# First layer's squares as TensorE products, and its first norm and layer 0 in one written plan

## The chip, the cores and the metric

The kernel runs on one core of a Trainium2 chip. The time is device microseconds of one execution of the whole program; a median of runs is given, and one execution is profiled besides. TensorE is PE in the rows (PEld is its weight load), VectorE is DVE, ScalarE is ACT, GpSimd is POOL; SP issues most of the DMAs. Each engine carries out its own list of instructions in the order in which they stand, and waits for the others by semaphores.

## The reference

Two transformer layers on 512 tokens of width 1024, all in fp32. Cut to what matters for the first layer:

```python
h = rmsnorm(x, attn_norm[layer])                       # x * rsqrt(mean(x*x) + 1e-6) * g
proj = h @ w_in_even[i]
fq, fk, fv, ff, dq, ckv, dkr, iq, ik, iw = jnp.split(proj, split_points, axis=-1)
log_f = jax.nn.log_sigmoid(ff + b_fox_f[i])
fox_out = fox_attention(fq, fk, fv, log_f)             # 8 causal heads with a decay
c_kv = rmsnorm(ckv, g_ckv[i])                          # rank 128
k_rope, iq, ik, dq = rope(...)                         # rotary part
# dsa: per query the 128 keys with the largest index score
score = einsum('bqh,bqhk->bqk', iw, relu(iq . ik)) * idx_scale
_, sel = lax.top_k(score, topk)                        # topk = 128
dsa_out = softmax(q . [c_kv, k_rope] over sel) @ c_kv @ w_uv    # 8 heads
x = x + concatenate([fox_out, dsa_out]) @ w_out_even[i]
x = x + conv_glu_ffn(rmsnorm(x, ffn_norm[layer]), ...)
```

The second layer has 16 heads of block-sparse attention and the same kind of feed-forward part; a norm ends the program.

## The kernel before

The residual stream lies transposed in SBUF: `xT[:, d]` holds features 128d to 128d+127 on the partitions and the 512 tokens along the row, for d from 0 to 7. Every matmul is made of three fp32r products (`mm3`, L171 to L173): a value is kept as a rounded high half (`xh`, `wh_...`) and the rest (`xl`, `wl_...`), and high by high, low by high and high by low are summed in PSUM. A projection such as `mm_fk1` is 8 feature blocks by 3 products, 24 matmuls of 128x512. The gain of the norm is put into `xh` and `xl` by `prep`; the factor 1/rms of a token is multiplied in afterwards, when the result is read out of PSUM (by RB, or by CR and SR, which are the rotary tables times RB). So projections can start before the norm is known, and their three `mm` banks in PSUM come free only after it.

A weight piece (`chunk`, 512 KB) comes by a DMA of SP, its high half is rounded on ACT (L160), and its low half is a subtraction, on DVE in one instruction (L166, 128x1024) or on POOL in four (L164, 128x256 each). Before the change that is one switch, `lo_on_pool`: DVE for the first four pieces, then POOL for all of layer 0's attention.

The first norm goes like this. ACT squares each `xT[:, d]` (L194, L197, L582), POOL and DVE add the eight squares (L198, L584, L585), PE transposes the sum (`st_n`, L204), DVE reduces it and finds the root by a bit trick and three Newton steps (L206 to L213), PE spreads it over the partitions (`bc_n`, L216), and ACT copies it to RB. The norm of ckv (`st_kv`, `bc_kv`) is of the same form.

The head of the program is in code order: `misc` (index keys, index weights, gates), `iq0`, `iq1`, `ckv`. Then the attention of layer 0 follows PLAN0, a string of steps, each of which writes its instructions on every engine: k, q and v are the projections of a head pair (0 to 3 are fox, 4 to 7 dsa), s00 the scores and the softmax of pair 0's first head, m00 its product with the values, i the index scores of a block of 128 queries, x a quarter of the selection for a block, o a part of the output projection. The selection (`select`, L631 and L632) finds the 128 largest scores by 16 rounds of MAX8 and MATCH_REPLACE8 for each of three query blocks, 48 rounds in all, on DVE; the masks `tmask1` to `tmask3` that come out are wanted by the dsa heads (`prt_d`, from s40 on). The score tiles of a head are four (128 to 512 keys), each read by one DVE instruction with its maximum (L360, `mx_f`, `mx_d`), and the PSUM banks for them are two (tag S), so that PE can be two tiles ahead of DVE.

Of the kernel before, what the change touches and what calls it, by code (L numbers as in the profile page):

```python
# [83 lines left out]
def hybrid_kernel(ctx: ExitStack, tc: tile.TileContext, xT_d, pos_d, const_d, vec_d, w_d, out_d, idx):  # L84
# [182 lines left out]
    def stack_k(y, nm, eng=V):  # L267

        out = []
        for n, t in zip("hl", halves(y, nm, eng)):  # L270
            b = big(f"{nm}_b{n}")
            move(b[LO], t[HI])
            move(b[HI], t[HI])
            move(t[HI], t[LO])
            out += [t, b]
        return out[0], out[1], out[2], out[3]
# [6 lines left out]

    def rope_angles():

        def fl(t):
            return t.rearrange("p b f -> p (b f)")

        def ang_tile(nm, k=1):
            return cp.tile([P, k * NB, 8], F32, name=f"ang_{nm}")  # L290
# [20 lines left out]
        n2 = rnd("n2", hi, BIG / TWO_PI)  # L311
        V.tensor_scalar(fl(t), fl(hi), M2[0], None, op0=OP.mult)
# [31 lines left out]
    def soft(nm, e, q, k, bias, decay=None):  # L344
# [4 lines left out]
        for i in range(NB):  # L349
# [50 lines left out]
    def v_group(nm, late=None):  # L400
# [3 lines left out]
        for c in range(2):  # L404
            wh, wl = chunk(f"{nm}{c}")
# [133 lines left out]
    def attention(pairs, plan, pieces):  # L539
# [3 lines left out]
        for step in plan.split():  # L543
            kind, n = step[0], step[1:]
# [19 lines left out]
    acc = sq_acc(0)  # L564
# [21 lines left out]
    w.append(chunk("iq1"))
    V.tensor_copy(selr[0:96, :P], const[0:96, C_SEL:C_SEL + P])
    V.tensor_copy(selr[96:128, :P], const[64:96, C_SEL:C_SEL + P])
    V.tensor_scalar(selr[:, P:], const[:, C_FSEL:C_FSEL + 8], 0.5, None, op0=OP.mult)
    rope_tables(cs)  # L590
    rstd_main(acc, "n0")
    rope_scaled()

    ym = rope(pmisc, "misc")
    ikh, ikl = big("ik_h"), big("ik_l")
    split(ikh[LO], ikl[LO], ym[LO])
    for t in (ikh, ikl):
        move(t[HI], t[LO])
    kr = big("kr")
    G.memset(kr[0:64].bitcast(F32), 0.0)  # L600
    split(kr[64:96], kr[96:128], ym[64:96])
    iwT = cp.tile([P, NB, 4], F32, name="iwT")
    t = ps("T", "iwps")
    for b in range(NB):
        PE.transpose(t[:, b * P:b * P + P], ym[:, b * P:b * P + P], ident)
    A.activation(iwT, t.rearrange("p (b c) -> p b c", b=NB)[:, :, 104:108], AF.Copy, scale=0.0625)
    iq = [stack_q(rope(proj(f"iq{h}", w[h]), f"iq{h}"), f"iq{h}") for h in range(2)]
# [28 lines left out]
    y = scaled(proj("ckv"), "ckv")  # L636
# [280 lines left out]
```

## Time and profile before

| | us |
|---|---|
| median of 3 runs (lowest, highest) | 1246.13 (1246.01, 1248.02) |
| profiled execution | 1245.54 |
| its span | 1243.8 |
| busy PE / DVE / ACT / POOL | 1211.7 / 812.3 / 556.2 / 357.5 |

The span goes from the first to the last instruction of the trace; the profiled execution's own time is 1.7 us longer. At 256 us of the span PE is in the output projection of layer 0's dsa heads; what comes behind is the feed-forward part of layer 0, layer 1 and the last norm. A view by stages (busy time of each engine in a stretch of the span) and the waits tell which engine ends last in a stage; the share of the whole span does not.

### The profile page before, as it was taken

Reading aid. Unit: us, or ns where it says so; the run is one execution under the profiler, and the core shown is the slowest. Engines: PE = TensorE matmul, PEld = TensorE weight load, DVE = VectorE, ACT = ScalarE, POOL = GpSimd, SP = SyncE. Lnnn points to the kernel's source line nnn. Section 1 sums busy time; section 2 is a strip of 40 time slices with the busy share of each in tenths; the row PEclk is TensorE's granted clock in tenths of the full one; section 3 lists DMA queues with packets and bytes.
Section 4 is the critical chain, followed back from the end, with each engine's and each line's share of the span. In section 5 each row is a group of like instructions: output and inputs, shape, how many; then the busy total and the mean of one; then the engine's idle time right before and its main releaser. Section 6 shows DMA issues by size and latency. Waiting matters only on the chain.

```text
span 1243.8 us, 16808 instructions
## 1 busy us (share of the span) xinstructions
PE 1211.7 (97%) x5996; PEld 1012.4 (81%) x5996; DVE 812.3 (65%) x1489; ACT 556.2 (45%) x969; POOL 357.5 (29%) x394
## 2 busy tenths in 40 slices
PE   6899999999999999999999999999999999999997
PEld 4778788888888888888888898888888888888886
DVE  7899987675555445554677787787655445554455
ACT  5574677644333333333434575575433323333234
POOL 3684667442111111111222332422221111111110
PEclk9999999999999999999999999999999999999998
DMA  5343435132332333323337424422232333333321
GB/s 196 103 132 88 126 98 132 56 100 83 107 102 89 98 102 95 92 92 95 106 99 193 124 77 119 120 65 84 85 102 85 102 103 102 101 87 101 102 85 68
DMA packets 57379, 127.24 MB, mean 102 GB/s; under 512 B 7584, under 2 KB 21024, under 8 KB 57296
## 3 DMA queue, kind: packets, MB, share of 16 engines
q1 hardware_dynamic: 56368, 124.81, 34.3%
q10 hardware_dynamic: 864, 1.17, 0.3%
q8 instruction: 47, 0.77, 0.3%
q14 instruction: 36, 0.29, 0.1%
q0 software_dynamic: 64, 0.20, 0.0%
HBM read 104.13 MB, written 2.10 MB: 85 GB/s over the span
## 4 chain that ended last, share of the span: by engine, by line
PE 85%; DVE 8%; issue 4%; ACT 1%; DMA 1%; POOL 0%; POOLq 0%; ACTq 0%; DVEq 0%
PE mm_g L172 6%; PE mm_g L171 6%; PE mm_g L173 6%; PE mm_u L171 6%; PE mm_u L172 6%; PE mm_u L173 6%; PE mm_d L171 6%; PE mm_d L172 6%; PE mm_d L173 6%; PE t_m L384 1%; DVE tmask L632 1%; DVE m L631 1%; PE mm_mk L171 1%; PE mm_mq L173 1%; PE mm_mk L173 1%
## 5 line engine op out<-in xcount | busy, mean ns | idle before, releaser
L446 POOL TENSOR_TENSOR cv<-cv,gs 128x512 f32<-128x512 f32 x44 | 57.2, 1299 | 546.0 <-ACT gs L445 546.0
L171 PE MATMUL mm_d<-a_h,wh_d 128*128 128x512 f32 (+1 forms) x384 | 142.8, 372 | 0.0
L172 PE MATMUL mm_d<-a_l,wh_d 128*128 128x512 f32 (+1 forms) x384 | 142.6, 371 | 0.0
L173 PE MATMUL mm_d<-a_h,wl_d 128*128 128x512 f32 (+1 forms) x384 | 142.6, 371 | 0.0
L515 DVE TENSOR_TENSOR us<-mm_u,cv 128x512 f32<-128x512 f32 x44 | 30.4, 692 | 168.1 <-PE mm_u L173 132.7
L171 PE MATMUL mm_u<-xh,wh_u 128*128 128x512 f32 x352 | 137.3, 390 | 0.0
L172 PE MATMUL mm_g<-xl,wh_g 128*128 128x512 f32 x352 | 137.2, 390 | 0.0
L173 PE MATMUL mm_u<-xh,wl_u 128*128 128x512 f32 x352 | 137.0, 389 | 0.0
L171 PE MATMUL mm_g<-xh,wh_g 128*128 128x512 f32 x352 | 137.0, 389 | 0.0
L173 PE MATMUL mm_g<-xh,wl_g 128*128 128x512 f32 x352 | 137.0, 389 | 0.0
L172 PE MATMUL mm_u<-xl,wh_u 128*128 128x512 f32 x352 | 136.9, 389 | 0.0
L160 ACT CAST wh_g<-raw_g 128x1024 fp32r<-128x1024 f32 x44 | 46.3, 1053 | 143.8 <-PE mm_g L172 141.6
L512 DVE TENSOR_TENSOR gs<-mm_g,RB 128x512 f32<-128x512 f32 x44 | 30.4, 691 | 118.2 <-PE mm_g L173 115.6
L140 ACT CAST wh_d<-raw_d 128x1024 fp32r<-128x1024 f32 x45 | 47.4, 1053 | 124.0 <-PE mm_u L172 103.7
L173 PEld LDWEIGHTS mm_d<-a_h,wl_d 128*128 128x128 f32 x384 | 72.3, 188 | 12.6
L171 PEld LDWEIGHTS mm_d<-a_h,wh_d 128*128 128x128 f32 x384 | 72.3, 188 | 12.5
L172 PEld LDWEIGHTS mm_d<-a_l,wh_d 128*128 128x128 f32 x384 | 72.3, 188 | 12.4
L172 PEld LDWEIGHTS mm_g<-xl,wh_g 128*128 128x128 f32 x352 | 66.1, 188 | 14.2 <-DVE xl L187 0.7
L173 PEld LDWEIGHTS mm_u<-xh,wl_u 128*128 128x128 f32 x352 | 66.1, 188 | 13.8
L171 PEld LDWEIGHTS mm_g<-xh,wh_g 128*128 128x128 f32 x352 | 66.1, 188 | 13.8
L173 PEld LDWEIGHTS mm_g<-xh,wl_g 128*128 128x128 f32 x352 | 66.1, 188 | 13.7
L171 PEld LDWEIGHTS mm_u<-xh,wh_u 128*128 128x128 f32 x352 | 66.1, 188 | 13.6
(778 smaller groups left out, 3059.3 us busy)
## 6 DMA issues: line engine op xcount, KB each, us to landing
raw_g<-in_w SPq DMA_DIRECT2D x44, 512.0 KB, 3.5
raw_u<-in_w SPq DMA_DIRECT2D x44, 512.0 KB, 3.6
raw_d<-in_w SPq DMA_DIRECT2D x41, 256.0 KB, 2.8
raw_d<-in_w SPq DMA_DIRECT2D x29, 192.0 KB, 2.7
raw_d<-in_w SPq DMA_DIRECT2D x34, 128.0 KB, 2.5
raw_oe<-in_w SPq DMA_DIRECT2D x8, 512.0 KB, 4.2
raw_mq<-in_w SPq DMA_DIRECT2D x8, 512.0 KB, 3.7
raw_mk<-in_w SPq DMA_DIRECT2D x8, 512.0 KB, 4.1
```

What stands on the lines that cost most here:

```text
L140: A.copy(dst_h, src)
L160: A.copy(wh, raw)
L171: PE.matmul(out, ah, bh, start=first, stop=False)
L172: PE.matmul(out, ah, bl, start=False, stop=False)
L173: PE.matmul(out, al, bh, start=False, stop=last)
L384: PE.transpose(t[:, n * P:n * P + P], probs[i][:, j * P:j * P + P], ident)
L446: G.tensor_tensor(cv, cv, gs, op=OP.mult)
L512: V.tensor_tensor(gs, og, RB, op=OP.mult)
L515: V.tensor_tensor(us, ou, cv, op=OP.mult)
L631: V.max(m8, sc)
L632: V.match_replace(sc, m8, sc, -3e38)
```

## The change

- **Squares on PE.** For each block of x, four fp32 products (not split) of a 128x128 block of `xT` with itself are summed over the 8 blocks into one PSUM bank (`st_n0`, 32 matmuls, L635 of the new code). The sums of squares of the tokens are on the diagonals; DVE multiplies by the identity and reduces. The squares on ACT and the sums on POOL and DVE are gone. The root is DVE's reciprocal, ACT's Sqrt and one Newton step.
- **ckv's norm.** The four transposes of its squares and the reduction are replaced by four fp32 products with a column of ones.
- **One plan.** The first norm, `misc`, `iq`, `ckv`, the gates and the whole attention of layer 0 are steps of PLAN0. A step has two digits and flags. New letters: p prepares a block, z squares it, a is the rotary tables, b `misc`, t the norm, w an early weight, r splits `misc`, j is `iq`, c `ckv`, f the gates, d the selectors. x is now an eighth of a selection (2 rounds). The projection fk1 stands before iq1 and ckv.
- **Flags.** g puts a weight's low half on POOL, otherwise it is on DVE; l puts the low half of a result (fq, iq, fk, o) on POOL; e builds the two stacked forms of q by half-height casts and subtractions and saves three DMAs (q2 and q5); w moves the other half of k. In layer 0 seven weights' low halves move from POOL to DVE (fv0's two, fq0, dq0 and three pieces of the output projection), and so do two of the four fk and three of the four o_f low halves.
- From the end of the dsa heads' output projection on (the feed-forward part of layer 0 and all behind it), the lists are the same as before.

```diff
 PLAN0 = (
-    "v0 i1 i2 k0 q0 i3 k1 s00 s01 q1 v2 x10 s10 m00 k2 s11 x11 m01 x12 q2 x13 x20 m10 k3 m11 k4 x21 s20 "
...
+    "p00 p01 p02 a00 p03 z00v z01 p04 p05 z02 p06 z03v p07 z04o z05o b00 z06o z07v a10 w00 a20 t00r j00ls "
+    "k10glw j10 r00 c00 v00 f00 i10 q00l i20 k00g d00 s00 i30 x10 x11 x12 q10g s01 s10 x13 s11 x14 v20g "
+    "m00 m01 k20glw m10 q20eg x20 k30g k40g x15 x21 x16 x22 x23 x24 x17 m11 x25 x30 x31 s20 x32 s21 x33 "
+    "q30g x34 m20 s30 s31 m21l x35 q40 k50gw v40 x26 x27 m30 x36 x37 k60w s40 s41 q50egl m31 q60g m40 s50 "
...
-        if lo_on_pool:
+        if pool:
...
+    def root(sums, y, h, n, flags, ms=None):
...
+        V.tensor_scalar(ms, sums, 1.0 / n, EPS, op0=OP.mult, op1=OP.add)
...
+        elif "r" in flags:
+            V.reciprocal(h, ms)
+            A.activation(y, h, AF.Sqrt)
...
+        for _ in range(1 if "p" in flags or "r" in flags else 3):
...
+    def sums_by_ones(st, sq, first, last):
+
+        nb = st.shape[1] // 2
+        for b in range(nb):
+            PE.matmul(st[:, 2 * b:2 * b + 2], sq[:, b * P:b * P + P], ones, start=first and b == 0, stop=last and b == nb - 1)
...
+    def stack_q(y, nm, flags):
+
+
+        if "e" in flags:
+            q = big(f"{nm}_a"), big(f"{nm}_b")
+            for t, r, o in ((q[0], LO, HI), (q[1], HI, LO)):
+                A.copy(t[r], y[r])
+                V.tensor_tensor(t[o], y[r], t[r].bitcast(F32), op=OP.subtract)
+            return q
+        h, l = halves(y, nm, G if "l" in flags else V)
...
-    for d in range(KT):
-        if d < 4:
-            square(d, acc)
...
+    def first_square(n, flags):
+
+
+        if n == 0:
+            x0["st"] = ps("T", "st_n0")
+        for b in range(NB):
+            s = slice(b * P, b * P + P)
+            PE.matmul(x0["st"][:, s], xT[:, n, s], xT[:, n, s], start=n == 0 and b == 0, stop=n == KT - 1 and b == NB - 1)
...
+    def first_scale(n, flags):
+        st = x0["st"]
+        ms, y, h = (col(f"{c}_n0", NB) for c in ("ms", "y", "h"))
+        d = tmp("diag")
+        V.tensor_tensor(d.rearrange("p (b c) -> p b c", b=NB), st.rearrange("p (b c) -> p b c", b=NB),
+                        ident.rearrange("p (b c) -> p b c", b=1).to_broadcast([P, NB, P]), op=OP.mult)
+        V.reduce_sum(ms, d.rearrange("p (b c) -> p b c", b=NB), axis=mybir.AxisListType.X)
+        root(ms, y, h, D, flags)
+        row_scale(y, spread(y, "n0"), "n0")
+        rope_scaled()
...
+    def latent(flags):
+
+        y = scaled(proj("ckv", x0.get("ckv"), "g" in flags, "S" if "s" in flags else "mm"), "ckv")
+        sq = tmp("sqkv")
+        A.activation(sq, y, AF.Square)
+        st = ps("T", "st_kv")[:, :2 * NB]
+        sums_by_ones(st, sq, True, True)
```

TensorE at the start of the program, before, and then after; `mm_misc` is the first projection and `st_n` the new squares:

```order
L171 MATMUL mm_misc<-xh,wh_misc 128x512
L172 MATMUL mm_misc<-xl,wh_misc 128x512
L173 MATMUL mm_misc<-xh,wl_misc 128x512
L171 MATMUL mm_misc<-xh,wh_misc 128x512
L172 MATMUL mm_misc<-xl,wh_misc 128x512
```

```order
L635 MATMUL st_n_146<-xT 128x128 x4
L174 MATMUL mm_misc<-xh,wh_misc 128x512
L635 MATMUL st_n_146<-xT 128x128 x4
L175 MATMUL mm_misc<-xl,wh_misc 128x512
L176 MATMUL mm_misc<-xh,wl_misc 128x512
L174 MATMUL mm_misc<-xh,wh_misc 128x512
L635 MATMUL st_n_146<-xT 128x128 x16
```

The squares, which need nothing but x itself, stand ahead of and between the first products of `misc`; the last eight follow its end.

VectorE where the first dsa head begins (step s40), before and then after; `tmask3_93` is the selection of the last query block, `mx_d00_0` and `prt_d00` the first dsa head's maxima and masked scores:

```order
L141 TENSOR_TENSOR pt_f30_1l_1923<-t_f30_1_1931,pt_f30_1h_1922 128x384
L360 ISA prt_d00_2027,mx_d00_0_2031<-s_d00_0_2028,cmask_83 128x128
L360 ISA mx_d00_0_2031 128x1
L360 ISA prt_d00_2027,mx_d00_1_2037<-s_d00_1_2034,tmask1_91 128x256
L360 ISA mx_d00_1_2037 128x1
L141 TENSOR_TENSOR dk1_l_1961<-mm_dk1_1955,dk1_h_1960 128x512
L141 TENSOR_TENSOR p3_0_1_95<-t_f30_2_1937,p3_0_0_94 128x256
L360 ISA prt_d00_2027,mx_d00_2_2043<-s_d00_2_2040,tmask2_92 128x384
```

```order
L712 MAX m8_3_1965<-tmask3_93 128x8
L452 TENSOR_TENSOR y_f3_1709<-y_f3_1709,o_f30_1920 64x512
L713 MATCH_REPLACE tmask3_93<-m8_3_1965,tmask3_93 128x512
L416 ISA prt_d00_1988,mx_d00_0_1992<-s_d00_0_1989,cmask_83 128x128
L416 ISA mx_d00_0_1992 128x1
L715 TENSOR_SCALAR tmask3_93<-tmask3_93 128x512
L416 ISA prt_d00_1988,mx_d00_1_1998<-s_d00_1_1995,tmask1_91 128x256
L416 ISA mx_d00_1_1998 128x1
L416 ISA prt_d00_1988,mx_d00_2_2004<-s_d00_2_2001,tmask2_92 128x384
```

The last round of the selection, which before stands some 40 instructions earlier, is now directly ahead of the first dsa scores on VectorE.

TensorE at the same step, before and then after; `s_d00_2` is the third score tile of the first dsa head, `mm_dq` a projection of a later pair's queries:

```order
L393 MATMUL o_f30_1919<-p3_0_0_94,fv1__942 128x256
L384 MATMUL t_f31_0_1990<-const_70,prt_f31_1765 128x128
L280 MATMUL s_d00_2_2040<-dk0_h_1505,dq0_a_1843 128x384
L281 MATMUL s_d00_2_2040<-dk0_l_1506,dq0_a_1843 128x384
L280 MATMUL s_d00_3_2046<-dk0_h_1505,dq0_a_1843 128x512
L281 MATMUL s_d00_3_2046<-dk0_l_1506,dq0_a_1843 128x512
```

```order
L440 MATMUL t_f31_1_2107<-const_70,prt_f31_1746 128x128 x3
L174 MATMUL mm_dq2_2144<-xh_74,wh_dq2_2136 128x512
L175 MATMUL mm_dq2_2144<-xl_75,wh_dq2_2136 128x512
L176 MATMUL mm_dq2_2144<-xh_74,wl_dq2_2137 128x512
L174 MATMUL mm_dq2_2144<-xh_74,wh_dq2_2136 128x512
L175 MATMUL mm_dq2_2144<-xl_75,wh_dq2_2136 128x512
L176 MATMUL mm_dq2_2144<-xh_74,wl_dq2_2137 128x512
L174 MATMUL mm_dq2_2144<-xh_74,wh_dq2_2136 128x512
L175 MATMUL mm_dq2_2144<-xl_75,wh_dq2_2136 128x512
L176 MATMUL mm_dq2_2144<-xh_74,wl_dq2_2137 128x512
L174 MATMUL mm_dq2_2144<-xh_74,wh_dq2_2136 128x512
L333 MATMUL s_d00_2_2001<-dk0_h_1427,dq0_a_1867 128x384
```

Ten of the 24 matmuls of `dq2`, which before come later, are now done before that tile.

## Rows read from the trace of the kernel before

**Rows 1.** The page: busy time of the engines, and busy tenths in 40 slices.
```profile
PE 1211.7 (97%) x5996; PEld 1012.4 (81%) x5996; DVE 812.3 (65%) x1489; ACT 556.2 (45%) x969; POOL 357.5 (29%) x394
...
DVE  7899987675555445554677787787655445554455
```
**Rows 2.** Stages: stretch, then busy us (instructions) per engine, granted clock, DMA share, GB/s.
```profile
44.50:75.00 30.50, 26.76 (x167) 23.21 (x166) 26.25 (x62) 20.08 (x34) 19.31 (x22) 1.00 0.39 105
75.00:100.00 25.00, 23.19 (x138) 19.71 (x138) 24.15 (x73) 14.89 (x30) 20.39 (x26) 1.00 0.57 153
100.00:125.00 25.00, 23.52 (x139) 20.04 (x138) 24.18 (x66) 12.76 (x32) 11.18 (x17) 1.00 0.32 87
125.00:157.00 32.00, 30.80 (x164) 25.09 (x163) 31.11 (x78) 18.62 (x41) 21.50 (x31) 1.00 0.49 128
157.00:175.30 18.30, 18.30 (x106) 15.59 (x105) 14.38 (x43) 13.75 (x36) 9.45 (x14) 1.00 0.24 68
175.30:256.00 80.70, 80.10 (x423) 65.30 (x423) 59.12 (x152) 55.67 (x133) 49.86 (x71) 1.00 0.37 96
```
**Rows 3.** Waits of PE, 0 to 256 us: total, times, longest.
```profile
PE mm_misc L172 <- DVE xl L187: 3.2, 2, 2.5
PE ix L280 <- ACT rl L620: 2.6, 2, 2.3
PE bc_n L216 <- DVE y_n L213: 2.2, 1, 2.2
...
PE s_f L356 <- DVE mx_f L360: 1.0, 2, 0.7
```
**Rows 4.** PE in order of time: start, length, instruction, [idle before].
```profile
6.68 0.79 PE L171 MATMUL mm_misc<-xh,wh_misc 128*128 128x512 f32 x1 [6.68 <-ACT wh_misc L140]
...
14.30 0.80 PE L172 MATMUL mm_misc<-xl,wh_misc 128*128 128x512 f32 x1 [2.54 <-DVE xl L187]
...
17.02 0.63 PE L172 MATMUL mm_misc<-xl,wh_misc 128*128 128x512 f32 x1
17.45 0.44 PE L173 MATMUL mm_misc<-xh,wl_misc 128*128 128x512 f32 x1
...
19.58 0.39 PE L173 MATMUL mm_misc<-xh,wl_misc 128*128 128x512 f32 x1
19.81 0.39 PE L171 MATMUL mm_iq<-xh,wh_iq 128*128 128x512 f32 x1
...
25.16 1.03 PE L338 MATMUL tabT<-const,exp_tab 128*128 128x128 f32 x8
```
**Rows 5.** Weight loads of unsplit fp32 products (two records each) at the end.
```profile
1234.66 0.30 PEld L785 LDWEIGHTS st_n<-ones,acc 128*128 128x128 f32 x2
1234.88 0.30 PEld L786 LDWEIGHTS st_n<-ones,sq 128*128 128x128 f32 x2
```
**Rows 6.** DVE in order of time.
```profile
8.06 1.25 DVE L294 TENSOR_SCALAR ang_n<-ang_r 128x32 f32<-128x32 f32 x1
9.23 0.17 DVE L295 TENSOR_SCALAR ang_n<-ang_n 128x32 f32<-128x32 f32 x1
...
27.86 0.17 DVE L207 TENSOR_SCALAR ms_n<-ms_n 128x4 f32<-128x4 f32 x1
28.06 0.17 DVE L208 TENSOR_SCALAR t_n<-ms_n 128x4 int32<-128x4 int32 x1
...
32.17 0.17 DVE L225 COPY rstd_n<-y_n 128x4 f32<-128x4 f32 x1
```
**Rows 7.** DVE where the counted stretch begins and ends.
```profile
43.89 0.68 DVE L240 TENSOR_TENSOR ry_iq<-ry_iq,rs_iq 128x512 f32<-128x512 f32 x1
44.49 0.68 DVE L245 TENSOR_TENSOR sc_ckv<-mm_ckv,RB 128x512 f32<-128x512 f32 x1
...
175.27 0.55 DVE L360 CUSTOM_DVE_ANT_0 prt_d<-s_d,tmask 128x384 f32<-128x384 f32 x1
```
**Rows 8.** DVE by groups, 44.5 to 175.3 us: busy, mean ns, idle before.
```profile
L141 DVE TENSOR_TENSOR fq_l<-sc_fq,fq_h 128x512 fp32r<-128x512 f32 x4 | 4.0, 1006 | 0.0
...
L141 DVE TENSOR_TENSOR dk_l<-mm_dk,dk_h 128x512 fp32r<-128x512 f32 x2 | 1.4, 684 | 0.0
```
**Rows 9.** ACT and a weight's low half on DVE, in order of time.
```profile
4.88 0.72 ACT L186 ACTIVATE xh<-xT,vec 128x512 fp32r<-128x512 f32 x1 [1.73 <-DMA vec<-in_vec]
...
20.85 1.28 ACT L323 ACT_TABLE_LOAD   x1
...
22.65 1.22 DVE L166 TENSOR_TENSOR wl_iq<-raw_iq,wh_iq 128x1024 fp32r<-128x1024 f32 x1
```

More of the change, by code (lines that the diff above doesn't have):

```diff
@@ L265, in stack_q, with stack_k @@
         return a, l
-    def stack_k(y, nm, eng=V):
+    def stack_k(y, nm, flags):
         out = []
-        for n, t in zip("hl", halves(y, nm, eng)):
+        one, two = (LO, HI) if "w" in flags else (HI, LO)
+        for n, t in zip("hl", halves(y, nm, G if "l" in flags else V)):
             b = big(f"{nm}_b{n}")
[L272 to L276, printed above, removed]
+            move(b[LO], t[one])
+            move(b[HI], t[one])
+            move(t[one], t[two])
+            out += [b, t] if "w" in flags else [t, b]
+        return out
     def scores(out, q, k, e, qs, w, first=True):
@@ L354, in soft @@
             if decay is not None:
-                sel, ck = decay
-                PE.matmul(s[:, :wm], sel.to_broadcast([P, P]), ck[:, :wm], start=True, stop=False)
+                PE.matmul(s[:, :wm], decay.to_broadcast([P, P]), misc["ck"][:, :wm], start=True, stop=False)
             scores(s[:, :wm], q, k, e, qs, wm, decay is None)
@@ L420, in v_group, with out_proj @@
         return v
-    def out_proj(nm, o, done=None, part=range(4)):
+    def out_proj(nm, o, done=None, part=range(4), pool=False):
         for dp in part:
-            wh, wl = chunk(f"{nm}{dp}")
+            wh, wl = chunk(f"{nm}{dp}", pool=pool)
             for e in range(2):
@@ L553, in attention @@
                 if e == 1:
-                    c["out"].append(halves(c["y"], f"o_{c['nm']}", c.get("lo", V)))
+                    c["out"].append(halves(c["y"], f"o_{c['nm']}", G if "l" in flags else V))
             else:
-                pieces[kind](int(n))
+                pieces[kind](int(n), flags)
     values = {}
@@ L586, in hybrid_kernel @@
[L586 to L600, printed above, removed]
@@ L601, in hybrid_kernel @@
-    split(kr[64:96], kr[96:128], ym[64:96])
-    iwT = cp.tile([P, NB, 4], F32, name="iwT")
[L603 to L607, printed above, removed]
+    x0 = {"misc": w}
+    def first_square(n, flags):
+        if n == 0:
+            x0["st"] = ps("T", "st_n0")
+        for b in range(NB):
+            s = slice(b * P, b * P + P)
+            PE.matmul(x0["st"][:, s], xT[:, n, s], xT[:, n, s], start=n == 0 and b == 0, stop=n == KT - 1 and b == NB - 1)
@@ new lines, in first_proj, with early_chunk, misc_split @@
+    def first_proj():
+        x0["misc"] = proj("misc", x0["misc"])
+    def early_chunk(n, flags):
+        nm = ("iq0", "iq1", "ckv")[n // 10]
+        x0[nm] = chunk(nm, pool="g" in flags)
+    iwT = cp.tile([P, NB, 4], F32, name="iwT")
+    misc, iq, ckv = {}, [None, None], []
+    def misc_split():
+        ym = misc["y"] = rope(x0["misc"], "misc")
+        ikh, ikl = big("ik_h"), big("ik_l")
+        split(ikh[LO], ikl[LO], ym[LO])
+        for t in (ikh, ikl):
+            move(t[HI], t[LO])
+        misc["ik"] = ikh, ikh, ikl, ikl
+        kr = misc["kr"] = big("kr")
+        G.memset(kr[0:64].bitcast(F32), 0.0)
+        split(kr[64:96], kr[96:128], ym[64:96])
+        t = ps("T", "iwps")
+        for b in range(NB):
+            PE.transpose(t[:, b * P:b * P + P], ym[:, b * P:b * P + P], ident)
+        A.activation(iwT, t.rearrange("p (b c) -> p b c", b=NB)[:, :, 104:108], AF.Copy, scale=0.0625)
@@ L661, in hybrid_kernel @@
-    V.tensor_tensor(ckt[R], lu[R], ck[R].bitcast(F32), op=OP.subtract)
-    for r in (0, 64):
-        A.copy(ck[r:r + 32], lu[R])
-        V.tensor_copy(ck[r + 32:r + 64], ckt[R])
-    lo_on_pool = True
+    def latent(flags):
[4 more added lines that the diff above has]
+        sums_by_ones(st, sq, True, True)
+        _, bc = rstd_by_ones(st, P, "kv", flags)
+        yn = tmp("ckvn")
+        V.scalar_tensor_tensor(yn, y, vec[:, V_GC:V_GC + 1], bc, op0=OP.mult, op1=OP.mult)
+        ckv.extend(halves(yn, "ckv"))
```

200 lines of the change are left out of this document (111 added, 89 removed), and 3 rows, old and new, of the table PLAN0.

## The prediction, made before the run

> **What bounds the kernel now.** I read the page first: PE is busy for 97% of the span, DVE for 65% [rows 1]. That would make every microsecond of PE work added a microsecond lost. But DVE's row of slices says otherwise for the start: slices 3 to 5 are at 9 [rows 1]. So I read the view by stages next [rows 2]. From 75 to 157 us DVE is busy for 24.15 of 25, 24.18 of 25 and 31.11 of 32 us; it has 2.6 us to spare in 82. PE idles 1.8, 1.5 and 1.2 us in the same stages. From 157 on PE is busy without a gap (18.30 of 18.30, then 80.10 of 80.70) and DVE is at 14.38 of 18.30. So three regimes: a head in which PE waits for data and for the norm, a middle in which DVE is full (the selection, the softmax, the low halves) and PE goes at its pace, and from about 157 us PE alone. Everything behind 256 us is the same list before and after, so only this first part counts, and the question is when PE gets to a fixed point of it. I take the third score tile of the first dsa head, read by DVE at 175.27 [rows 7].
>
> The waits of PE in the head are 3.2 us for `xl`, 2.2 us for the norm (`bc_n`), and a start at 6.68 [rows 3, 4]. In the middle they are small ones, for DVE's maxima (1.0) and for ACT (2.6) [rows 3].
>
> **The head.** `misc` takes PE from 6.68 to 19.81 [rows 4]. At the later step of 0.23 us (19.58 to 19.81) its 24 matmuls would take 5.5 us. The rest is waits and a slow clock: up to 17.45 the step is 0.43 us, the lower of the two levels (1.2 GHz), then 0.23 [rows 4]. PE had run without a gap since 14.30, some 3 us, when the clock rose [rows 4].
>
> Added: 32 fp32 products. Nothing of that shape is in the trace. The nearest row is the unsplit fp32 product of the last norm: two records each, 0.22 us from one product to the next (1234.66 to 1234.88), though with two columns only [rows 5]. For 128 columns the tables' transposes give 1.03/8 = 0.13 us a pass [rows 4]. Two passes are 0.22 to 0.26; I take 0.24, 7.7 us in all. At the lower clock it would be twice that. At no cost they can't be, since PE is in order; four passes would be 0.47 each, 15 us.
>
> The Trainium skill ("FP8 and Floating Point Precision", "TensorE Precision Notes") speaks against the change here: "True FP32: 4 passes through PE array". By that the squares would take the 15 us of the upper bound. The trace shows two records per product, so I go by two and keep four as a rival.
>
> What they displace: the squares need only x, which ACT reads from 4.88 on [rows 9], so PE starts 1.8 us earlier and the products fill the waits for `xl`. PE then runs without a gap from about 4.9, and if the clock rises after some 3 us of that, as before, it does so near 8 to 9 instead of 17.45. Sum: 3.5 us at half speed give 1.75 of work; the other 11.4 of 7.7 + 5.5 at full speed end at 19.8; with a microsecond of waits left, 21, against 19.81. If the clock rose as late as before, 22 to 23.
>
> The norm itself: before, DVE's reduction ends at 27.8 and the root at 32.17, steps of 0.20 us each and some stretched, and PE waits 2.2 [rows 3, 6]. After: the multiplication and the reduction (0.7 each), six small steps, at most one table load of 1.28 [rows 9], and one more DVE weight ahead (1.22) [rows 9]: about 5 us from 21, so 26. PE gets to `bc_n` after three quarters of `iq0` and the tables (4.1 + 1.0), at 26.1. So that wait goes, or is a few tenths. The squares of ACT and POOL's sums are off the chain; nothing else is waiting for them. Three `mm` banks hold `misc`, `iq0` and `fk1` until RB is there; `iq1` wants one at 33.5, seven microseconds later, so this costs nothing unless the norm is that late.
>
> Then `fk1`, `iq1`, `ckv`, 5.5 us each: PE ends `ckv` at 21 + 5.5 + 1.0 + 0.5 + 16.5 = 44.5; up to 46.5 with the late clock. Before, DVE takes ckv's result at 44.49 [rows 7], without `fk1` done. I put DVE at 45.3 there: 0.8 us later than before, with 5.5 us more of PE work done.
>
> **The middle, by DVE.** From ckv's result (44.49) to the fixed point (175.27) are 130.8 us, of which DVE is busy 120.1 and idle 10.7 (the five stages of [rows 2] added up). How does its list change between these two instructions? By the order of its instructions: in come 2 weight halves (`fq0`, `dq0`; 1.14 each net of overlap, from 1.22 [rows 9]), 2 `fk`, 2 `o_f` and 1 `dk` low halves, 1 `y_f`, and `ik_l` and `kr`, which stood ahead before, at 0.60 a step (43.89 to 44.49 [rows 7]), and one smaller one (0.3): 7.4. Out go `iq_l`, `sc_fk1`, ckv's reduction and a small step: 2.0. The eighths of the selection are interleaved more finely: some 22 MAX8 or MATCH_REPLACE8 no longer stand right behind the one they need. A step that depends on its neighbour takes 0.20 (27.86 to 28.06) against about 0.10 for others [rows 6], so 22 x 0.115 = 2.5 less. Net **+2.9**.
>
> POOL has 28 weight quarters fewer. What does DVE gain? The trace shows DVE stretched while POOL works: `fq_l`, from SBUF, takes 1006 ns against 684 ns for the same shape from PSUM [rows 8], and in the head a 32-element step takes 1.25 us against 0.17 [rows 6]. Four `fq_l` are 1.3 us; with the mask and gate instructions perhaps 4.5 in all. POOL has about a quarter of its weight work less; I take **-1.5**, bounds 0 and -4.5.
>
> The Trainium skill ("SBUF — State Buffer", the section on the two sides of SBUF) calls this port pair "an exclusive lock, not a bandwidth split", and has DVE blocked only with two SBUF inputs or in a fast mode. The 1.25 us step has one input. By the lock every POOL piece removed frees a whole DVE wait, and the sum would be nearer to -4.5.
>
> Idle time: of the 10.7 us, 4.25 lie in the gates' stage and 3.9 after 157, where DVE has finished the selection and waits for PE [rows 2]. In the new plan the last selection round stands directly ahead of the dsa scores, so DVE is never ahead and the 3.9 go; PE is further ahead in the gates, so I leave 6.5 in all: **-4.2**, bounds -7 and +5. Together 130.8 + 2.9 - 1.5 - 4.2 = 128.0, and the fixed point is at 45.3 + 128.0 = 173.3, 2.0 us earlier than before.
>
> **Behind it, PE alone.** PE has then done more than before: ten matmuls of `dq2` (2.3), two of `dk2` and a few of `t_f` and `o_f` (1.1), together 3.4. DVE has 59 us of work in the next 81 [rows 2], so PE sets the end, and those 3.4 us come off. The remaining low halves that come to DVE (three output pieces, 1.2 each) are hidden by that; without the cover they would cost 3.7.
>
> Sum: -2.0 - 3.4 = **-5.4** on the profiled 1245.54, that is 1240.1. The span is 1.7 shorter than this time, before as after. The profiled execution is 0.6 below the median of 1246.13, so I predict 1240.7 for the median.
>
> **The rivals.**
> (A) The forecast, DVE paces the middle: 1237 to 1243.6.
> (B) DVE has enough slack and PE's waits go. PE idles 8.2 us in the 130.8 [rows 2], and 1.1 us less work stands there (`fk1` out, 3.4 and the small norm in). PE starts 1.4 later: 1.4 - 8.2 - 1.1 - 3.4 = -11.3, 1234.8. For it: PE is ahead at every handover by instruction counts. Against: DVE's list got longer, and DVE was full already.
> (C) The gain is eaten in the head: four passes per product, or the late clock with a late norm. Squares of 15 us put ckv at 52, DVE at 52.5; some of DVE's idle time is then used up (125.5 instead of 128.0): 178.0, +2.7 - 3.4 = -0.7, 1245.4: no change.
> (D) Slower: DVE and PE in lock-step over the 32 fox score tiles. With two banks for scores, DVE waits for a tile and PE for a maximum in turn. PE's waits for maxima are 0.3 to 0.7 us a time [rows 3]. At 0.3 for each of 32 tiles, DVE loses 9.6 us: +4.2, 1250.3. It decides from 0.25 a tile. Against: before, DVE lost 2.6 us in 82 under the same two banks.
>
> **How the numbers follow.** A 0.47, B 0.14, C 0.21, D 0.18. A measurement of this kernel can tell about 0.2% (2.5 us) from no change. A and B are faster (0.61), C is the same (0.21), D slower (0.18). The range goes from 1233.0 (B) to 1249.5: about the upper half of D and a little of B are left out. A's own range is 1237 to 1243.6.
>
> **What would show it.** Right: `st_n0` in two records of 0.11 to 0.13 each at the full clock; clock up before 12 us; no wait at `bc_n`; ckv's result on DVE at 44.5 to 46.5; DVE busy over 95% from 60 to 170; the third dsa tile read at about 173; the same point of the output projection 5 us earlier. Wrong: the squares at 15 us (C); PE waiting on `mx_f` for over 8 us in all (D); PE without waits in the middle (B); or a wait in the head that I have at nothing, such as `iq1` for a free bank.

## The result, and the profile after

| | before | after |
|---|---|---|
| median, us (lowest, highest) | 1246.07 (1245.34, 1248.02) | 1238.93 (1238.71, 1240.82) |
| profiled execution / its span | 1245.54 / 1243.8 | 1239.11 / 1237.0 |

The ratio of the medians is 0.9939, with an interval of 0.9926 to 0.9952: 7.1 us faster. The forecast of 1240.7 was 1.8 us too high; the range and the sign held. On the profiled execution it was 1.0 too high (1240.1 for 1239.11); the rest is how far that execution lay from its median, 0.5 below before and 0.2 above after.

The page of the changed kernel, engines and DVE's row of slices, against [rows 1]:

```profile
PE 1215.3 (98%) x6060; PEld 1021.3 (83%) x6060; DVE 811.2 (66%) x1489; ACT 555.3 (45%) x965; POOL 333.7 (27%) x361
...
DVE  7799998775554555445687877777655445554455
```

PE has 64 records more and 3.6 us more busy time in a span that is 6.8 shorter, so what went is PE's waiting. The stages show where. Stretch, then busy us (instructions) of PE, PE's weight load, DVE, ACT and POOL, granted clock, DMA share, GB/s; the changed kernel, its first two stages, those that answer [rows 2], and from the third dsa tile to the first matmul of `mm_oe__3`, a fixed point of the last output projection that the list of both kernels has:

```profile
0.00:20.00 20.00, 15.57 (x88) 14.28 (x88) 13.97 (x45) 12.00 (x17) 7.08 (x17) 1.00 0.70 249
20.00:44.51 24.51, 23.83 (x113) 19.54 (x111) 17.13 (x35) 9.76 (x13) 7.99 (x6) 1.00 0.52 143
44.51:173.30 128.79, 122.54 (x715) 104.52 (x716) 121.47 (x325) 80.12 (x174) 68.94 (x92) 1.00 0.41 109
75.00:100.00 25.00, 22.28 (x150) 20.11 (x149) 24.65 (x78) 14.09 (x30) 16.28 (x21) 1.00 0.35 90
100.00:125.00 25.00, 24.77 (x134) 20.55 (x134) 24.35 (x66) 16.13 (x39) 16.89 (x26) 1.00 0.34 90
125.00:157.00 32.00, 32.00 (x177) 26.86 (x176) 30.70 (x85) 21.33 (x55) 12.50 (x20) 1.00 0.48 125
173.30:247.90 74.60, 73.77 (x400) 60.99 (x398) 61.39 (x151) 55.20 (x131) 39.18 (x55) 1.00 0.29 82
```

The same stretches of the kernel before:

```profile
0.00:20.00 20.00, 9.79 (x25) 6.45 (x26) 14.26 (x41) 13.85 (x23) 7.53 (x16) 1.00 0.66 226
20.00:44.49 24.49, 20.78 (x105) 16.52 (x105) 21.73 (x48) 9.24 (x13) 11.48 (x13) 1.00 0.35 107
44.49:175.27 130.78, 122.54 (x707) 103.65 (x705) 120.04 (x318) 80.09 (x171) 81.80 (x106) 1.00 0.42 111
175.27:254.44 79.17, 78.57 (x416) 63.98 (x416) 58.46 (x151) 55.03 (x131) 48.33 (x69) 1.00 0.38 98
```

Up to ckv's result (44.5 in both) PE is busy for 39.4 us instead of 30.6: the squares and all of `fk1` fit into what was waiting and slow clock. (The column of the granted clock stands at 1.00 in both first stretches, although the steps of PE there are at half rate at first, up to 17.45 us before and about 9.7 after; so in the head the level is read from the steps.) From there to the third dsa tile PE's busy time is the same to the hundredth, 122.54, and its idle time falls from 8.24 to 6.25: that is the whole gain of 2.0. Behind the tile PE has 16 matmuls and 4.8 us of busy time less, and the fixed point comes 4.57 sooner after it (74.60 against 79.17). In all it lies 6.54 earlier (247.90, 254.44): counted from the start of the program PE has 10.6 us less idle time (12.2 for 22.7) and 4.0 more busy time. The remaining 0.3 of the span comes behind it.

### The profile page after: what moved, and what is told of

It is laid out like the page before. It is cut to its first block, busy times and chain, and to the rows that moved or that the text cites. A ratio compares the mean times of both kernels' runs of the same rounds, so it can differ in the third digit from the quotient of the medians.

```text
span 1237.0 us, 16862 instructions
## 1 busy us (share of the span) xinstructions
PE 1215.3 (98%) x6060; PEld 1021.3 (83%) x6060; DVE 811.2 (66%) x1489; ACT 555.3 (45%) x965; POOL 333.7 (27%) x361
## 4 chain that ended last, share of the span: by engine, by line
PE 87%; DVE 7%; issue 4%; ACT 1%; DMA 1%; POOL 1%; POOLq 0%; ACTq 0%; DVEq 0%
PE mm_g L174 6%; PE mm_g L175 6%; PE mm_g L176 6%; PE mm_u L174 6%; PE mm_u L176 6%; PE mm_u L175 6%; PE mm_d L176 6%; PE mm_d L174 6%; PE mm_d L175 6%; PE t_m L440 1%; DVE tmask L713 1%; DVE m L712 1%; PE mm_mk L174 1%; PE mm_mq L176 1%; PE mm_mk L175 1%
## 5 line engine op out<-in xcount | busy, mean ns | idle before, releaser
L175 PEld LDWEIGHTS mm_d<-a_l,wh_d 128*128 128x128 f32 x384 | 72.3, 188 | 12.6
L176 PEld LDWEIGHTS mm_d<-a_h,wl_d 128*128 128x128 f32 x384 | 72.3, 188 | 12.5
L175 PEld LDWEIGHTS mm_u<-xl,wh_u 128*128 128x128 f32 x352 | 66.1, 188 | 13.6
## 6 DMA issues: line engine op xcount, KB each, us to landing
raw_d<-in_w SPq DMA_DIRECT2D x34, 128.0 KB, 2.5
```

Source lines behind the costliest of these rows:

```text
L175: PE.matmul(out, ah, bl, start=False, stop=False)
L176: PE.matmul(out, al, bh, start=False, stop=last)
```

## The experiments

Two of them keep the changed kernel's order of instructions fixed on every engine (by ordering-only dependencies); in the others the edit also moves other instructions, because the written plan places them anew. That turned out to matter. Three parts of the change were not run alone: ckv's norm, the stacked q (flag e), and the finer eighths of the selection. For each kernel one row says how it goes from 20 us to `mm_oe__3`: the length, and PE's busy time in it. For the changed kernel and then the kernel before:

```profile
20.00:247.90 227.90, 220.14 (x1227) 185.05 (x1225) 199.99 (x510) 145.08 (x317) 116.11 (x152) 1.00 0.38 104
```

```profile
20.00:254.44 234.44, 221.90 (x1224) 184.15 (x1224) 200.24 (x513) 144.37 (x315) 141.62 (x186) 1.00 0.40 106
```

Length less busy time is idle time: 7.8 us after, 12.5 before.

**The squares alone** (`squares_alone`): the old kernel and its old plan, with the first norm of the change.

```diff
     for d in range(KT):
         prep(d, 0, None)
+        for b in range(NB):
+            s = slice(b * P, b * P + P)
+            PE.matmul(st[:, s], xT[:, d, s], xT[:, d, s], ...)
...
-    rstd_main(acc, "n0")
```

> The kernel before with the first norm of the change alone (32 fp32 products, diagonal, reciprocal and Sqrt); the plan and the flags are the old ones. Theory (VectorE paces the middle, so TensorE's added work in the head costs nothing as long as ckv gets to VectorE no later): the norm is known 5 to 6 us earlier, ckv's result is read at about 42 instead of 44.5, the rest follows: about -2.5 us, 1243 to 1244.5. Rival (TensorE's work counts, the gain comes from the new plan): the 7.5 us of products are added, less 5 us of waits: +2 to +5 us, 1248 to 1251.

Measured: 1247.78, ratio 1.0012 (1.0003 to 1.0021), 1.4 slower than before. ckv's result is 4.4 us earlier (40.06) and the third dsa tile at 172.52, 2.75 earlier; the fixed point is 2.9 later. From tile to fixed point:

```profile
172.52:257.35 84.83, 81.41 (x419) 65.27 (x418) 59.17 (x149) 55.28 (x132) 49.30 (x70) 0.98 0.33 88
```

Against 79.17 before: 2.8 us more idle and 2.8 us more busy time for three matmuls more, with the granted clock at 0.98. The time is just below the second number and far from the first, but neither theory holds: 2.75 of the head's 4.4 us reach the dsa heads, and there they are lost to waits and a low clock (a granted clock of 0.50 from 189.7 to 193.3 us, behind a wait of 1.7).

**The plan with the old norm** (`old_norm`): squares on ACT, sums on POOL and DVE, the old root.

```diff
-            PE.matmul(x0["st"][:, s], xT[:, n, s], xT[:, n, s], ...)
+        A.activation(s, xT[:, n], AF.Square)
+        V.tensor_tensor(x0["acc2"], x0["acc2"], s, op=OP.add)
...
+        rstd_main(x0["acc"], "n0")
```

> The changed kernel with the first norm of before (squares on ACT, sums on GpSimd and VectorE, transposes, bit trick and three Newton steps); the plan is the new one. Theory: RB comes at 33 to 34 instead of 26.5, iq1 waits some 2 us for a PSUM bank, ckv gets to VectorE 1 to 2 us later than in the changed kernel: 1240 to 1241.5, so most of the gain is the plan's. Rival (the squares bring the gain): 1245 to 1246.

Measured: 1243.51, ratio 0.9976 (0.9967 to 0.9986): 2.9 faster than before, 4.6 slower than after, and above the expected number: ckv's result comes 5.3 us later than in the changed kernel (49.80), not 1 to 2. DVE does the additions of the squares ahead of `wl_iq`, which ends the wait of PE; PE in order of time, start, length, instruction, [idle before]:

```profile
23.95 0.50 PE L176 MATMUL mm_iq<-xh,wl_iq 128*128 128x512 f32 x1 [3.15 <-DVE wl_iq L169]
24.29 0.40 PE L174 MATMUL mm_iq<-xh,wh_iq 128*128 128x512 f32 x1
...
25.30 0.63 PE L174 MATMUL mm_iq<-xh,wh_iq 128*128 128x512 f32 x1
```

After the wait of 3.15 us the first two matmuls are still quick; by 24.9 the step is 0.43 us instead of 0.23 and stays there until 27.9. That is the lower clock level (the granted clock of 25 to 27 us is 0.50), which the kernels before and after show at the program's start alone. The squares on PE save DVE this queue. The two parts do not add: +1.4 alone, -2.9 alone, -7.1 together.

**The squares twice** (`double_squares`): every product repeated, the mean halved.

```diff
-        for b in range(NB):
+        for b in range(2 * NB):
```

> The changed kernel with every one of the 32 products made twice (and the mean taken over twice the width): 7.5 us more of TensorE in the head, nothing else. Theory: ckv gets to VectorE some 7 us later, at about 51.5; a part of VectorE's idle time in the middle (7.3 us) absorbs 2 to 3 of it: +4 to +6 us over the changed kernel, 1243 to 1245, the price my four-pass rival would have had. Rival (the head has slack, TensorE is far ahead of VectorE there): within 1 us of the changed kernel.

Measured: 1246.22, ratio 1.0000 (0.9991 to 1.0010), 7.3 above after. The fixed point moves by 6.95. Of the work added in the head nothing is absorbed by the middle; I had expected DVE's reserve to take some.

**Less and more of DVE's selection, order held** (`fix_cut`, `fix_long`): the last four rounds read 64 columns, 8.0 us less; the maxima of the last eight rounds of two blocks read twice, 5.3 us more (the lengths of MAX8 and MATCH_REPLACE8 add up to 52.6 us after, to 44.6 and 57.9 here).

```diff
+            part = sc[:, :64] if r >= 12 else sc        # fix_cut
...
+            if i < 3 and r >= 8:                        # fix_long
+                V.max(m8, sc.rearrange(...).to_broadcast([P, 2, P * (i + 1)]))
```

> The changed kernel with the last 4 of the 16 selection rounds of each query block done over 64 columns instead of 256 to 512 (that part of the selection is left out). Every engine's order of instructions is held to that of the changed kernel, only the 24 instructions are shorter: 8.0 us less of VectorE before the third dsa tile, by 1 column per 0.96 GHz cycle as the durations of the other rounds give it. Theory (VectorE paces the middle): the third dsa tile is read 5 to 7 us earlier than at 173.3 and the time is 1232.5 to 1234.5. Rival (TensorE paces the middle, or the two pass waits to and fro): the tile at 172 to 173.3 and 1238 to 1239.

> The changed kernel with the last 8 MAX8 of the first two selected query blocks reading their row twice (512 and 768 columns instead of 256 and 384; their result is the wrong one, that part of the selection is spoilt). The order of every engine is held to that of the changed kernel: 5.3 us more of VectorE in the middle. Theory: VectorE has 2 us of true waits left there, so the third dsa tile comes 4 to 5.3 us later and the time is 1242.5 to 1244.5. Rival (TensorE paces): within 1 us of 1238.9.

Measured: `fix_cut` 1237.33, ratio 0.9924 (0.9909 to 0.9939), 1.6 below after; `fix_long` 1241.75, ratio 0.9958 (0.9941 to 0.9975), 2.8 above; each lies between its two numbers. The intervals touch that of the changed kernel (0.9926 to 0.9952), so the times alone show little; the reading rests on the tile in one trace of each. Stages of `fix_cut`, up to its third dsa tile:

```profile
75.00:100.00 25.00, 22.96 (x157) 20.97 (x156) 24.09 (x81) 15.02 (x33) 17.08 (x23) 1.00 0.35 88
100.00:125.00 25.00, 24.88 (x129) 20.38 (x128) 24.23 (x65) 16.41 (x39) 15.71 (x24) 1.00 0.33 91
125.00:157.00 32.00, 32.00 (x181) 27.07 (x180) 29.51 (x87) 21.26 (x55) 13.56 (x21) 1.00 0.53 136
157.00:171.43 14.43, 13.52 (x70) 10.83 (x69) 10.69 (x33) 7.01 (x15) 6.34 (x10) 1.00 0.53 120
```

With 8 us less, DVE has room from 125 us on (29.51 of 32, 10.69 of 14.43), and PE is at 32.00 of 32: the tile comes only 1.9 earlier, at 171.43, of which 0.3 already lies ahead of ckv's result (44.21). With 5.3 more the tile is at 177.05, 3.75 later, of which 0.9 lies ahead of ckv's result (45.38). So in the changed kernel DVE and PE are level: a slower DVE costs over half of what is added (2.9 of 5.3), a quicker one gives a fifth of what is taken (1.6 of 8.0). "DVE paces the middle" holds in the one direction only.

**A shorter selection, order free** (`short_select`): every fourth round left out.

```diff
+            if r % 4 == 3:
+                continue
```

> The changed kernel with 12 instead of 16 rounds of the selection for each query block, so each query keeps 96 keys instead of 128 (that part of the computation is left out): 12 MAX8 and 12 MATCH_REPLACE8 fewer, about 14 us of VectorE between 60 and 170 us. Theory (VectorE paces the middle): the third dsa score tile comes 5 to 8 us earlier, until TensorE itself is full: 1231 to 1234. Rival (TensorE paces the middle, VectorE follows): 1238 to 1239, as the changed kernel.

Measured: 1254.0, ratio 1.0059 (1.0044 to 1.0074). With 14 us of selection less it is 15 us slower than after. The placing of everything else changed with it; PE waits 3.4 for `fk_h` and in two waits 3.4 for ACT, and its busy time to the fixed point is 227.12 instead of 220.14. It answers nothing on DVE, and was the reason for the two above.

**Weights' and results' low halves back on POOL** (`wl_pool`: seven weights; `lo_pool`: two fk and three o_f; `v00_pool`: fv0's two weights alone; `k00_lo`: the low half of fk0 alone).

```diff
-  q00l   v00   q40   o00   o10   o30      # wl_pool; v00_pool: v00 alone
+  q00lg  v00g  q40g  o00g  o10g  o30g
-  k00g   m01   k30g   m11   m31           # lo_pool; k00_lo: k00 alone
+  k00gl  m01l  k30gl  m11l  m31l
```

> The changed kernel with the low halves of all seven weights back on GpSimd (fv0's two, fq0, dq0, three of the output projection). The scheduler orders this kernel anew. Theory: VectorE has 2.4 us less in the middle and 2.4 less ahead of it, and GpSimd's 28 pieces more stretch VectorE's other steps by 1 to 2 us: 1237 to 1239. Rival (every GpSimd piece holds VectorE up for its whole length, 28 x 0.8 us, half of them in the middle): 1242 to 1248.

> The changed kernel with the low halves of two fk and three o_f back on GpSimd (flag l on k00, k30, m01, m11, m31). The scheduler orders this kernel anew. Theory: VectorE has 3 us less in the middle, less 1 us of stretching: 1236.5 to 1238. Rival (GpSimd's slower subtraction, 1.3 to 1.4 us, comes onto the path of the scores that wait for it, or holds VectorE up): 1239 to 1241.

> The changed kernel with the low halves of fv0's two weights back on GpSimd (flag g on v00), every engine's order else nearly untouched. Theory: the eight pieces stand ahead of misc's rotary product on GpSimd, misc's result comes 3 us later, TensorE waits 3.2 instead of 0.7 us for it (near 44 us) and runs some 3 us at the lower clock: ckv reaches VectorE at 47 to 48.5 instead of 44.5, and the time is 1242 to 1245. Rival (VectorE gains 2.4 us ahead of the middle, and it paces): 1236.5 to 1238.

> The changed kernel with one low half more on GpSimd, that of fk0 (flag l on k00). Theory of the wait and the clock (a wait of TensorE of over 3 us is followed by some 3 us at the lower clock, and no wait of the changed kernel is that long): fk0's low half comes 2 us later, the three moves that follow it too, TensorE waits 3.5 us instead of 1.2 at the first scores (near 82 us), the clock falls for about 3 us behind it, together 3 to 5 us: 1242 to 1244. Rival (all of the 11 us that the five l flags cost came from the scheduler's other order or from the other four): 1238.5 to 1240.

Measured, against the 1238.93 of the changed kernel: `wl_pool` 1251.32 (ratio to before 1.0037, 1.0024 to 1.0050), `lo_pool` 1250.0 (1.0026, 1.0017 to 1.0036), `v00_pool` 1243.52 (0.9973, 0.9963 to 0.9984), `k00_lo` 1254.0 (1.0046, 1.0029 to 1.0063). `v00_pool` does as expected (its profiled execution, at 1246.0, is the slowest of its runs); the other three lie above both of their numbers and cost far more than the DVE time that they save. The rows to the fixed point, first `v00_pool`, then `k00_lo`:

```profile
20.00:254.44 234.44, 223.68 (x1225) 188.50 (x1225) 198.82 (x509) 145.80 (x318) 121.16 (x160) 0.98 0.38 103
```

```profile
20.00:262.99 242.99, 226.85 (x1225) 189.90 (x1225) 201.51 (x510) 145.67 (x318) 117.23 (x153) 0.97 0.36 99
```

Both parts grow, here and in the other two (to 259.51 in `wl_pool`, PE busy 226.00; to 258.22 in `lo_pool`, PE busy 223.75): 3.0 to 8.4 us more idle, and 3.5 to 6.7 us more busy time for the same work, at a granted clock of 0.97 to 0.99. Where the idle time starts is seen best in the two with a single edit. `v00_pool`, POOL, then PE:

```profile
40.85 3.71 POOL L167 TENSOR_TENSOR wl_fv<-raw_fv,wh_fv 128x256 fp32r<-128x256 f32 x4
44.53 1.25 POOL L283 TENSOR_TENSOR rs_misc<-rs_misc,SR 128x512 f32<-128x512 f32 x1
```

```profile
46.66 1.09 PE L684 MATMUL iwps<-const,ry_misc 128*128 128x128 f32 x4 [3.17 <-DVE ry_misc L284]
...
47.97 0.63 PE L175 MATMUL mm_ckv<-xl,wh_ckv 128*128 128x512 f32 x1
```

The four pieces of `wl_fv` stand ahead of `rs_misc` on POOL. `rs_misc`, at 40.48 in the changed kernel, starts at 44.53; DVE's `ry_misc` and PE's `iwps` wait for it, and with `iwps` the last three matmuls of ckv and everything behind. The wait is 3.17 instead of 0.7. The granted clock falls to 0.50 at 45.4, still within the wait, and stays there until 52.4.

`k00_lo`: POOL, then SP's queue of DMAs, then PE:

```profile
75.85 2.83 POOL L167 TENSOR_TENSOR wl_fv<-raw_fv,wh_fv 128x256 fp32r<-128x256 f32 x4
78.64 1.29 POOL L146 TENSOR_TENSOR fk_l<-sc_fk,fk_h 128x512 fp32r<-128x512 f32 x1
```

```profile
79.95 1.10 SPq L300 DMA_DIRECT2D fk_bl<-fk_l  x2
...
81.78 0.46 SPq L300 DMA_DIRECT2D fk_h<-fk_h  x1
```

```profile
86.36 0.75 PE L333 MATMUL s_f<-fk_h,fq_a 128*128 128x256 f32 x2 [3.46 <-DMA fk_h<-fk_h]
86.91 0.41 PE L176 MATMUL mm_fv__0_1033<-wh_fv,xl 128*128 128x256 f32 x1
```

And the changed kernel at the same place, DVE, SP and PE:

```profile
76.17 1.17 DVE L146 TENSOR_TENSOR fk_l<-sc_fk,fk_h 128x512 fp32r<-128x512 f32 x1
```

```profile
77.38 1.10 SPq L300 DMA_DIRECT2D fk_bl<-fk_l  x2
...
79.20 0.46 SPq L300 DMA_DIRECT2D fk_h<-fk_h  x1
```

```profile
83.51 0.47 PE L333 MATMUL s_f<-fk_h,fq_a 128*128 128x256 f32 x2 [1.18 <-DMA fk_h<-fk_h]
83.83 0.28 PE L175 MATMUL mm_fv__0_1033<-wl_fv,xh 128*128 128x256 f32 x1
```

One low half 2.5 us later (78.64 for 76.17; 0.5 of it is there at ckv's result already) holds the DMA of `fk_bl` in SP's queue, and with it the DMA of `fk_h` behind it, by 2.6; the wait of PE grows from 1.18 to 3.46, and the step of a 256-column matmul goes from 0.11 to 0.21 us until 89. Wait (2.3 more) and clock (half of some 3.3 us) explain about 4 of the 15 us. Two more waits, 2.3 us for DVE's `dv` at 163 and 1.7 for POOL's `prt_d` at 226, have slow stretches with them as well. The one at `dv` shows in the granted clock, 0.81 here and 1.00 in every stage of the changed kernel:

```profile
157.00:175.00 18.00, 15.06 (x67) 11.92 (x66) 13.48 (x32) 8.28 (x20) 10.24 (x14) 0.81 0.38 96
```

In all the granted clock is 0.50 in three stretches: 86.3 to 89.8, 164.8 to 171.8 and 229.7 to 233.2. PE is busy for about 12.6 us of them; half of that, 6.3, is an estimate of what the clock cost, and is nearly the whole 6.7 us of PE's added busy time. With some 5.3 us that the three waits are longer than in the changed kernel, 11 to 12 of the 15 us have a place. Why the two later waits arise, with many other instructions placed anew, I have not traced.

**The same with work to fill the wait** (`k00_fill`): `k00_lo` with 14 products of no use ahead of that head's first score, to keep PE busy.

```diff
+            if nm == "f00" and i == 0:
+                for n in range(14):
+                    PE.matmul(s, xh[:, n % KT, :P], xh[:, n % KT], start=True, stop=True)
```

> The kernel k00_lo with 14 more TensorE products of 512 columns (3.2 us, their result is overwritten) ahead of the first scores, so that TensorE works where it would wait. Theory (the lower clock behind a long wait is a cost of its own): the wait shrinks to under 1 us, the scores come at the same time, the clock stays up, and the time is 1 to 2 us less than k00_lo's although TensorE does more. Rival (only the wait itself counts): the same as k00_lo or up to 3 us more.

Measured: 1253.25, ratio 1.0049 (1.0034 to 1.0064), like `k00_lo`. The products ran at 73.34, nine microseconds ahead of the wait, which stayed (3.87, with the slow matmuls behind it). So it says nothing on whether a filled wait would keep the clock; that is open.

**fk1 late** (`fk1_late`): the projection back behind the start of the selection.

```diff
-... "k10glw j10 r00 ... x12 q10g s01 ...
+... "j10 r00 ... x12 k10glw q10g s01 ...
```

> The changed kernel with fk1's projection back behind the selection's start (before q1) instead of ahead of iq1. Theory (TensorE and VectorE are both nearly full in the middle, so work done early counts): ckv reaches VectorE at about 40 instead of 44.5, but 5.5 us of TensorE's work come back into the middle: 1239 to 1242. Rival (VectorE alone paces): 4 us faster, 1234.5 to 1236.

Measured: 1253.26, ratio 1.0057 (1.0040 to 1.0075), far above both numbers. ckv's result comes at 40.49, 4 us earlier, as expected. At its new place fk1's low half stands on POOL behind three additions of the index scores. POOL, then PE:

```profile
91.97 4.40 POOL L706 TENSOR_TENSOR tmask<-rl,tmask 128x512 f32<-128x512 f32 x3
96.32 1.35 POOL L146 TENSOR_TENSOR fk_l<-sc_fk,fk_h 128x512 fp32r<-128x512 f32 x1
```

```profile
102.53 0.55 PE L333 MATMUL s_f<-fk_bh,fq_a 128*128 128x256 f32 x1 [3.50 <-issue]
```

SP's queue stands from 92.4 until that half is there (97.70), with four more DMAs behind it, and PE, which needs `fq_a` (issued at 98.90 and 100.18), waits 3.50 for the scores; the granted clock of 100 to 125 us is 0.86. The run shows that fk1's early place keeps its low half out of the way; it does not measure what 5.5 us of PE work ahead of ckv are worth by themselves.

## Why the prediction was right, and where it was not

**The head: right, and better by 0.8 us.** PE at its start and around the norm, against [rows 4]:

```profile
4.43 2.07 PE L635 MATMUL st_n<-xT 128*128 128x128 f32 x8 [4.43 <-DMA xT<-in_x]
...
9.29 0.63 PE L174 MATMUL mm_misc<-xh,wh_misc 128*128 128x512 f32 x1
9.72 4.02 PE L635 MATMUL st_n<-xT 128*128 128x128 f32 x32
13.49 0.48 PE L175 MATMUL mm_misc<-xl,wh_misc 128*128 128x512 f32 x1
...
18.17 1.95 PE L635 MATMUL st_n<-xT 128*128 128x128 f32 x16
...
25.40 0.60 PE L235 MATMUL bc_n<-const,y_n 128*128 128x128 f32 x4
```

A product leaves two records: 16 of them, eight products, take 1.95, 0.244 each where I took 0.24. So the price was right, but I read it wrongly: I called a record a pass. The split matmuls of 512 columns step by 0.23 us at the full clock [rows 4], 0.058 for 128 columns; a product of 0.236 to 0.244 is four of those, in two records. The 0.47 us and 15 us of rival C counted each pass at twice that, and C falls. The Trainium skill ("FP8 and Floating Point Precision", "TensorE Precision Notes") states four passes for true FP32. The trace agrees with the Trainium skill in time, 0.244 us against 4 x 0.058 = 0.23, so it did not speak against the change. The step at 9.29 is still 0.43; the 32 records that start at 9.72 take 3.77 up to the next matmul, 0.118 each, so the clock was up by about 9.7, against 17.45 before and 8 to 9 forecast. PE had been without a gap since 4.43, that is for 5.3 us; the "some 3 us" that I took from the one rise before did not hold. Squares and `misc` end at 20.1 (I had 21) and `bc_n` starts without a wait. The norm's last step on DVE ends 0.3 us ahead of it, so this wait is gone by little.

**The middle: the sum right, its mechanism half right.** DVE against [rows 7], and by groups (busy, mean ns) against [rows 8]:

```profile
44.51 0.68 DVE L289 TENSOR_TENSOR sc_ckv<-mm_ckv,RB 128x512 f32<-128x512 f32 x1
...
173.30 0.56 DVE L416 CUSTOM_DVE_ANT_0 prt_d<-s_d,tmask 128x384 f32<-128x384 f32 x1
```

```profile
L146 DVE TENSOR_TENSOR fq_l<-sc_fq,fq_h 128x512 fp32r<-128x512 f32 x2 | 2.4, 1208 | 0.0
```

The tile came at 173.30, the very number forecast, because two errors cancel: ckv 0.8 earlier (44.51 for 45.3), and the stretch 0.8 longer (128.8 for 128.0). In it DVE has 1.4 us more work, which is 2.9 less 1.5 as summed, and 7.3 us idle where I left 6.5. The trace bears the terms out. Added up by their lengths, the instructions that came and went are 5.0 us more (5.4 by the list); those in both kernels are 1.3 shorter (the -1.5 for quieter ports); and neighbours overlap by 2.2 more (the -2.5 for the finer selection). Three steps that close a mask lost 2.0 us, where I had looked to `fq_l`; `dq_l` (0.8) and `fq_l` (0.4) grew. The three, before and then after (busy, mean ns):

```profile
L634 DVE TENSOR_SCALAR tmask<-tmask 128x256 f32<-128x256 f32 (+2 forms) x3 | 3.2, 1066 | 0.0
```

```profile
L715 DVE TENSOR_SCALAR tmask<-tmask 128x256 f32<-128x256 f32 (+2 forms) x3 | 1.2, 404 | 0.0
```

The longest of them, 1.42 us at 86.28 before, runs beside POOL's `fk_l` (86.26 to 87.56). With POOL at 68.94 us instead of 81.80 not every step got shorter: the two `fq_l` that are left take 1208 ns on average, one 682 and one 1735, against 1006.

What failed is the step "PE goes at DVE's pace". PE's busy time is unchanged and the 2.0 us gained are 2.0 of its 8.2 us of idle time, the quantity that rival B counted; `fix_cut` shows PE as the next limit at once. The two forecasts were two sides of one balance, and A's number was nearer because PE's waits shrank by a quarter and did not vanish.

**Behind the tile: sign right, mis-sized.** I took 3.4 us off; the runs show 4.6. PE's busy time there is 4.8 less. The ten matmuls of `dq2`, the two of `dk2`, and three each of `o_f` and `t_f` are gone from the stretch as counted, and one each of `mm_oe` and `s_d` is in; by their steps that is about 3.4, and the remaining 1.2 I cannot put on a line. The low halves that came to DVE are hidden (DVE 61.39 of 74.60).

**The rivals.** D, lock-step at the maxima, did not come. PE's waits for 0 to 256 us, against [rows 3]:

```profile
PE st_n L635 <- DMA xT<-in_x: 4.4, 1, 4.4
PE ix L333 <- ACT rl L701: 1.6, 1, 1.6
PE s_f L412 <- DVE mx_f L416: 1.5, 2, 0.9
PE s_f L333 <- DMA fk_h<-fk_h: 1.2, 1, 1.2
```

1.5 us for `mx_f` in all, against the 9.6 that D asked for; the one at `mm_dk` for DVE is 0.9. But the slower side had another danger, for which I had no rival. Of nine kernels in which the changed plan was placed anew, six are slower than the kernel before, two (`old_norm`, `v00_pool`) lose 4.6 of the 7.1, and in each of these eight a wait of 3 to 4 us stands with a stretch of half clock; the ninth, `double_squares`, has no such stretch and costs what was added. The changed kernel has no wait above 1.6 us behind its start and a granted clock of 1.00 in every stage. This, more than any single term, separates it from its neighbours. It does not explain the 7.1 us: the kernel before has no stretch of half clock behind its start either.

## What to carry to other kernels

When an in-order engine is nearly full, ask of each edit which instruction it puts ahead of which on the helper engines and in the DMA queue: a low half that is 2.5 us late on POOL came with a loss of far more than the DVE time that it saved. Parts of a change whose gains meet in one queue cannot be priced alone (+1.4 and -2.9 gave -7.1), and an experiment in which a planner moves the rest tests the planner: hold the order fixed. Look for unchanged busy time first; the idle time that is left then says what was gained.

## What the runs showed of the hardware

- After waits inside a full stretch PE ran at the lower of its two clock levels (1.2 GHz): 3.15 us idle, then quick matmuls for 0.6 us, then a step of 0.43 for 3 us (`old_norm`); 3.46 idle, then half clock from the start (`k00_lo`). The granted clock in these stretches is 0.50. It was seen with waits of 3.1 to 3.9 us in eight kernels, and with several of 1.5 to 2.9 (2.35 in `wl_pool`, 2.89 in `lo_pool`); the waits of 2.2 and 2.3 us of the kernel before [rows 3], 2.6 in `double_squares` and the 1.6 us for `rl` after had no slow stretch behind them. Busy time to the fixed point rose by 2 to 7 us in these kernels. That the wait is the cause is argued from the sequence alone; the run that was to fill one did not.
- An fp32 product of 128x128 took two records of 0.118 to 0.122 us at full clock, together as long as four times 128 columns of the split matmuls (0.23 us for 512).
- DVE's steps out of SBUF vary beside POOL's work: the three `tmask` steps took 1066 ns on average before and 404 after, `fq_l` 1006 (four) and 1208 (two) with POOL less busy. So the stretch of a DVE instruction does not follow POOL's total; for `fq_l`'s shape out of PSUM it was 684 ns [rows 8].
